# w_up: the tile endings cut into six one-engine steps, spread half a tile apart

## The chip, the core and the metric

The kernel runs on one core of one Trainium2 chip. Its time is device microseconds (us) from start to end of one execution. Before the change it is 2656.06 us, the median of three runs (2653.28, 2656.06 and 2662.95).

## What is computed

Two transformer-like blocks on x of 256 tokens by 2048 features, in fp32. Only one part of the first block matters here, the convolutional feed-forward layer:

```python
def _conv_ffn(h, w_up, conv_w, conv_b, w_down):
    u = h @ w_up                                # 256 x 2048 @ 2048 x 11264
    up = jnp.pad(u, ((0, 0), (CONV_WIDTH - 1, 0), (0, 0)))
    y = conv_b
    for j in range(CONV_WIDTH):                 # 3 taps along the tokens
        y = y + conv_w[j] * up[:, j:j + T]
    val, gate = jnp.split(y, 2, axis=-1)
    return (jax.nn.silu(gate) * val) @ w_down   # 256 x 5632 @ 5632 x 2048
```

## The kernel before, in words

**Weights.** Every large product streams its weights in pieces of 128 x 1024 fp32 values (512 KB). For each piece SyncE's queue (SP) issues a DMA into a raw buffer (L568). Then ACT writes the high half of the piece, rounded to fp32r (L587, through the helper `act`, L423), and DVE writes the low half, the piece less its high half (L588, through `tt`, L426). TensorE multiplies both. A program written by hand sets the order: `next` (L617) hands out a prepared piece and, before that, prepares pieces until four are ready, so that the piece prepared at one call is multiplied three calls later. A buffer ring of 13 slots (5 raw, 4 high, 4 low) serves the stream, so a new high half takes the slot of a piece that TensorE has just left.

Between the weight pieces of w_up and w_down the plan (`mix`, L533) lays 96 pieces of the modulation weights `w_ada`, two for every five. DVE alone works on those: one scalar_tensor_tensor (STT) of 128x1024 each (`_ada`, L628, through `stt`, L433). After each sixteen of them come a few small matmuls with the constant `con` (L763 to L778).

**w_up.** `block_ffn` (L1782) makes 88 tiles of 128 features by 256 tokens: 44 values j of the loop, each with i = 0 (the value) and i = 1 (the gate). `form_b` (L781) makes one tile from two pieces. A piece is 8 pairs of matmuls: the high weights on 512 columns (high and low input side by side) and the low weights on 256 columns. The 32 matmuls of a tile go into one PSUM bank, of which `pm` (L413) rotates three. The first two tiles come from `form_b2` (L798), which prepares the input at the same time.

**The ending of a tile** stands right behind its matmuls in the program, L1803 to L1814. It goes back and forth between two engines: ACT copies the upper 256 columns of the bank into `u`, DVE adds the lower 256 (`join`, L451); ACT makes `z`, the last tap with its bias (Identity, the only ACT operation of shape `s<-s,vec`); DVE adds the other two taps (STTs of 255 and 254 columns). For i = 1, ACT then takes the Silu and DVE multiplies into `act`. Each of the two engines carries out its instructions in the order of the program. So the high half that `next` makes for the following tile stands on ACT behind this ending, and the low half stands on DVE behind it. The working slot `y` is taken at each j and given back at the end of i = 1.

Around that, `bg` (L457) runs background generators (the rope tables early in w_up) and the late ends of `_ada`. After w_up comes w_down in the same function (L1823 on), in pieces of 24 matmuls of 512 columns, and later the second block, whose `win2` tiles use `form_b` too, with lighter endings.

Of the kernel before, what the change touches and what calls it, by code (L numbers as in the profile page):

```python
# [13 lines left out]
AF = mybir.ActivationFunctionType  # L14
ALU = mybir.AluOpType
# [4 lines left out]
T = 256  # L20
# [3 lines left out]
NFF = DFF // P  # L24
# [203 lines left out]
class Clock:  # L228
# [7 lines left out]
    def __init__(self):  # L236
        self.at = dict.fromkeys(("PE", "DVE", "ACT", "POOL", "SP"), 0.0)
        self.done, self.read = {}, {}
        self.columns = {}
        self.on = True  # L240
# [100 lines left out]
class Kern:  # L341
# [5 lines left out]
    def __init__(self, ctx, tc, a, out):  # L347
        self.clock = Clock()
        self.nc, self.a, self.out = Engines(self.clock, tc.nc), a, out
        self.timed = []  # L350
        p = self.const = ctx.enter_context(tc.tile_pool(name="const", bufs=1))
        self.vec = p.tile([P, NV], F32, name="vec")
        self.con = p.tile([P, NC_], F32, name="con")
        self.cs = p.tile([P, 32], F32, name="cs")
        self.mcol = p.tile([P, 6, 16], F32, name="mcol")
        self.scb = p.tile([P, 2, 16], F32, name="scb")
        self.mu1 = p.tile([P, 27], F32, name="mu1")
        self.ka1 = p.tile([P, 8], F32, name="ka1")
        self.st = p.tile([P, 16], F32, name="st")
        self.ssq = p.tile([P, 2, 2, 4], F32, name="ssq")  # L360
        self.epsr = p.tile([P, 2], F32, name="epsr")
        self.slots = ctx.enter_context(tc.tile_pool(name="slots", bufs=1))
        self.free_list = list(range(self.NSLOT))

        self.stream = list(range(self.NSLOT, self.NSLOT + self.RAW + self.HI + self.LO))
        self.used = []
        self.held = {}
        self.who, self.own, self.mixers = None, {}, []
        self.ps = ctx.enter_context(tc.tile_pool(name="ps", bufs=1, space=PSUM))
        self.ring_m, self.ring_g = [0, 1, 2], [3, 4, 5, 6]  # L370
        self.dram = ctx.enter_context(tc.tile_pool(name="dram", bufs=1, space=bass.MemoryType.DRAM))
        self.gens = []
        self.late = []
        self.flags = set()
# [242 lines left out]
    def next(self, name, lead=None, keep=False):  # L617
        if not keep:
            self.give(*self.used)
            self.used = []  # L620
        self.prefetch((self.lead if lead is None else lead) + 1)
        key, h, l = self.ready.pop(0)
        assert key == name, (key, name)
        self.used += [h, l]
        return h, l
# [155 lines left out]
    def form_b(self, name, nk, x):  # L781


        o = self.pm()
        for q in range(nk // 8):
            wh, wl = self.next(name)
            for kk in range(8):
                self.prod_b(o, wh, wl, x, kk, 8 * q + kk, nk)
            if q < nk // 8 - 1:
                self.bg()  # L790
        return o
# [429 lines left out]
    def step(self, g):  # L1221

        c = self.clock
        self.who = g[2]
        c.last = 0.0
        r = next(g[1], "end")
        self.who = None
        if r == "end":
            self.gens.remove(g)
            self.mixers.remove(g[2])  # L1230
        elif r == "wait":
            return False
        elif r != "go":
            g[0] = r or c.last
        return True
# [546 lines left out]
    def block_ffn(self):  # L1782
        nc = self.nc
        rs = self.st[:, 8:10]
        first, xs = self.form_b2("wup")
        x = self.by2(xs)
        act = [self.take() for _ in range(11)]
        av = self.at4(act)
        parts = {}

        def split(i):
            if i < 44:
                parts[i] = self.take(F32R), self.take(F32R)
                self.hl(*parts[i], act[i % 11])
                if i >= 33:
                    self.give(act[i % 11])

        for j in range(NFF):
            if j >= NFF - 2:
                split(j - NFF + 2)  # L1800
            y = self.take()
            for i in range(2):
                o = self.form_b("wup", 16, x) if j else first[i]  # L1803
                n = j + NFF * i
                z = y[:, i * T:(i + 1) * T]
                u = y[:, 512 + i * T:512 + (i + 1) * T]
                self.bg()
                self.join(u, o)
                self.act(z, u, AF.Identity, scale=self.v("cw2", n), bias=self.v("cb", n))
                self.stt(z[:, 1:], u[:, :T - 1], self.v("cw1", n), z[:, 1:], ALU.mult, ALU.add)  # L1810
                self.stt(z[:, 2:], u[:, :T - 2], self.v("cw0", n), z[:, 2:], ALU.mult, ALU.add)
            self.act(y[:, 512:768], y[:, T:512], AF.Silu)
            self.tt(av(j), y[:, 0:T], y[:, 512:768])
            self.give(y)  # L1814
            if j == 1:
                self.gens.append(self.rope_tables())
        self.give(*xs)
        gf = [self.take() for _ in range(2)]
        for h in range(2):
            nc.scalar.dma_start(out=gf[h], in_=self.a["nfg"][:, h * 1024:(h + 1) * 1024].to_broadcast([P, 1024]))  # L1820
        y = [self.take() for _ in range(4)]
        self.f = []
        for n in range(4):  # L1823
            o = [self.pm(), self.pm()]
            if n == 1:
                self.scale, self.shift = self.mod_affine("gpre", 5, 4)
            xh = lambda k: parts[11 * n + k // 4][0][:, (k % 4) * T:(k % 4 + 1) * T]
            xl = lambda k: parts[11 * n + k // 4][1][:, (k % 4) * T:(k % 4 + 1) * T]
            for q in range(22 if n < 3 else 18):
                i = 11 * n + q // 2  # L1830
                if (n, q) == (3, 14):
                    self.lend(-8)
                    self.lead = self.AHEAD
                if q % 2 == 0:
                    split(i + 2)
                wh, wl = self.next("wdn")
                self.piece_a(o, wh, wl, xh, xl, 2 * q, NFF)
                if q % 2:
                    self.give(*parts.pop(i))
                self.bg()  # L1840
            gate = lambda tt: self.add_gated(o, n, 5, tt, y, gf)
            if n == 2:
                self.warm(AF.Sqrt)
            if n < 3:
                gate(0)
                gate(1)
                self.turn_soon(y, n)

        self.y, self.rf = y, self.st[:, 4:6]

        def stats(tt):
            sl = slice(tt, tt + 1)
            vw = self.st[:, 0:2]
            nc.vector.tensor_reduce(out=vw, in_=self.ssq[:, :, tt], axis=AX.X, op=ALU.add)  # L1854
            v, w, e = vw[:, 0:1], vw[:, 1:2], self.st[:, 2:3]

            self.ts(e, v, EPS / D, EPS * EPS, ALU.mult, ALU.add)
            self.stt(w, w, 1.0 / D, e, ALU.mult, ALU.add)
            nc.vector.reciprocal(w, w)  # L1859
            self.act(rs[:, sl], w, AF.Sqrt)  # L1860
            self.diag(rs, tt)
            self.rstd(self.rf[:, sl], v, D)

        self.finish_a("wdn", o, xh, xl, NFF, gate, stats, lambda tt: self.turn(y[3], 3, self.scale, tt))
        for i in (42, 43):
            self.give(*parts.pop(i))
        self.give(self.row.pop((5, 0)), self.row.pop((5, 1)), *gf)
# [337 lines left out]
```

## Time and profile before

| | |
|---|---|
| median of 3 runs | 2656.06 us |
| the profiled execution's own time | 2659.07 us |
| its span in the profile | 2657.3 us |
| TensorE (PE) busy | 2552.5 us, 96% of the span |
| DVE busy | 1853.7 us, 70% |
| ACT busy | 1258.4 us, 47% |
| mean granted TensorE clock | 0.985 of full speed |

PE is the matmul side of TensorE and PEld its weight loads, which overlap the matmuls. The ends of matmuls in the profile are modelled and overlap one another; a high busy share of PE therefore does not say that it runs at its own pace. In a group of instructions the last part reads: busy us, mean ns of one, then the engine's idle time just before them and what ended most of it.

### The profile page before, as it was taken

How to read it: one execution, taken by the hardware profiler on the slowest of the kernel's cores; microseconds unless marked ns; L12 is line 12 of the kernel's file. 1: busy time of each engine (PE TensorE's matmuls, PEld its weight loads, DVE VectorE, ACT ScalarE, POOL GpSimd, SP SyncE). 2: the span in 40 equal slices, each digit the busy share in tenths (PEclk: the TensorE clock that was granted, in tenths of full speed). 3: DMA queues.
4: the chain of work that ended last, by engine and by line, in shares of the span. 5: the costliest groups of instructions: out<-in, count | busy, mean ns of one | idle time of the engine just before them, and what ended most of it. 6: DMA issues, size and time to landing. Idle time of an engine off the chain costs nothing.

```text
span 2657.3 us, 40136 instructions
## 1 busy us (share of the span) xinstructions
PE 2552.5 (96%) x15788; PEld 2119.8 (80%) x15788; DVE 1853.7 (70%) x2598; ACT 1258.4 (47%) x1923; POOL 89.1 (3%) x120
## 2 busy tenths in 40 slices
PE   6999999988999999999998999999999999999998
PEld 3777777667788888878887888888888888888887
DVE  3548955678788887888876556666787688566664
ACT  3363322345444444455665554444444444554443
POOL 0001032001000000000001000000000000000000
PEclk8999999998999999999998999999999999999999
DMA  9956764865677777777764654445666666555574
GB/s 372 388 171 208 265 210 160 280 201 174 236 239 255 240 249 236 247 270 269 267 217 146 200 193 156 143 151 198 216 202 215 222 200 199 181 187 189 190 242 143
DMA packets 168633, 579.65 MB, mean 218 GB/s; under 512 B 17914, under 2 KB 18298, under 8 KB 168444
## 3 DMA queue, kind: packets, MB, share of 16 engines
q1 hardware_dynamic: 163424, 561.88, 62.6%
q10 hardware_dynamic: 3916, 11.54, 1.3%
q0 software_dynamic: 1104, 3.67, 0.4%
q8 instruction: 123, 2.02, 0.3%
q14 instruction: 66, 0.54, 0.1%
HBM read 572.82 MB, written 4.19 MB: 217 GB/s over the span
## 4 chain that ended last, share of the span: by engine, by line
PE 55%; DVE 1%; ACT 0%; issue 0%; DVEq 0%; ACTq 0%
PE b L436 55%; PE b L439 1%; DVE s L426 0%; DVE s L433 0%; ACT s L423 0%; DVEq L2185 0%; ACT st L423 0%; DVE s L1875 0%; DVE st L430 0%; DVE s L430 0%; DVE st L916 0%; DVE st L1859 0%; DVE st L1854 0%; DVE st L433 0%; DVE st L1320 0%
## 5 line engine op out<-in xcount | busy, mean ns | idle before, releaser
L436 PE MATMUL b<-s,s 128*128 128x512 f32 (+1 forms) x10496 | 2010.1, 352 | 37.1 <-DVE s L426 23.2
L436 PEld LDWEIGHTS b<-s,s 128*128 128x128 f32 x10496 | 1688.1, 189 | 335.0 <-DVE s L426 38.2
L426 DVE TENSOR_TENSOR s<-s,s 128x1024 fp32r<-128x1024 f32 (+4 forms) x906 | 983.9, 1107 | 316.5 <-ACT s L423 299.8
L423 ACT ACTIVATE s<-s 128x1024 fp32r<-128x1024 f32 (+3 forms) x954 | 839.3, 913 | 481.2 <-PE b L436 170.4
L327 PE MATMUL b<-s,s 128*128 128x256 f32 (+6 forms) x4480 | 457.0, 306 | 48.4 <-DMA s<-in_w_ada 23.0
L327 PEld LDWEIGHTS b<-s,s 128*128 128x128 f32 (+3 forms) x4480 | 346.9, 159 | 154.0 <-issue 66.0
L423 ACT ACTIVATE s<-b 128x256 f32<-128x256 f32 (+2 forms) x338 | 134.3, 407 | 320.9 <-PE b L436 264.3
L426 DVE TENSOR_TENSOR s<-b,s 128x256 f32<-128x256 f32 (+1 forms) x324 | 143.7, 447 | 122.4 <-ACT s L423 100.0
L327 DVE TENSOR_TENSOR s<-s,s 128x1024 fp32r<-128x1024 f32 (+5 forms) x119 | 129.8, 1105 | 80.2 <-ACT s L327 76.6
L423 ACT ACTIVATE s<-s,vec 128x256 f32<-128x256 f32 x88 | 53.0, 602 | 224.8 <-DVE s L426 224.8
L327 ACT ACTIVATE s<-s 128x1024 fp32r<-128x1024 f32 (+6 forms) x112 | 108.1, 981 | 99.2 <-DVE s L327 37.0
L433 DVE SCALAR_TENSOR_TENSOR s<-s,cs,s 128x1024 f32<-128x1024 f32 x120 | 153.3, 1277 | 0.0
L327 ACT ACTIVATE s<-b 128x512 f32<-128x512 f32 (+1 forms) x105 | 52.5, 539 | 186.8 <-PE b L327 177.2
L433 DVE SCALAR_TENSOR_TENSOR s<-s,vec 128x255 f32<-128x255 f32 (+1 forms) x176 | 85.1, 484 | 62.1 <-ACT s L423 59.0
L327 DVE SCALAR_TENSOR_TENSOR s<-s,cs,s 128x1024 f32<-128x1024 f32 x51 | 65.7, 1288 | 14.1 <-DMA s<-in_w_ada 13.4
L426 DVE TENSOR_TENSOR s<-s 128x256 f32<-128x256 f32 x94 | 39.9, 425 | 26.9 <-ACT s L423 25.3
L426 POOL TENSOR_TENSOR s<-s,s 128x512 f32<-128x512 f32 x14 | 19.8, 1443 | 1014.3 <-ACT s L423 903.1
L433 DVE SCALAR_TENSOR_TENSOR s<-b,s 128x384 f32<-128x384 f32 x40 | 22.1, 553 | 36.6 <-PE b L436 36.6
L327 DVE TENSOR_TENSOR s<-b,s 128x256 f32<-128x256 f32 (+2 forms) x68 | 28.3, 465 | 24.8 <-PE b L327 20.9
L327 DVE TENSOR_TENSOR s<-s,b 128x512 f32<-128x512 f32 (+1 forms) x47 | 25.3, 559 | 20.0 <-PE b L327 19.7
L2039 POOL DMA_DIRECT2D s<-in_gpost x2 | 1.1, 533 | 1119.5 <-PE b L436 1119.5
L327 PEld LDWEIGHTS b<-con,s 128*128 128x128 f32 (+1 forms) x288 | 24.6, 158 | 9.8 <-ACT s L327 7.2
(115 smaller groups left out, 626.1 us busy)
## 6 DMA issues: line engine op xcount, KB each, us to landing
s<-in_win SPq DMA_DIRECT2D x302, 512.0 KB, 3.6
s<-in_w_ada SPq DMA_DIRECT2D x288, 512.0 KB, 5.0
s<-in_wup SPq DMA_DIRECT2D x176, 512.0 KB, 4.8
s<-in_wdn SPq DMA_DIRECT2D x88, 512.0 KB, 4.8
s<-in_win2v SPq DMA_DIRECT2D x48, 512.0 KB, 3.5
s<-in_wina SPq DMA_DIRECT2D x32, 512.0 KB, 10.6
s<-in_wout SPq DMA_DIRECT2D x32, 512.0 KB, 4.6
s<-in_wmp SPq DMA_DIRECT2D x32, 512.0 KB, 3.8
```

Of the source, the lines that this page charges most:

```text
L327: r = f(*a, **k)
L423: return self.nc.scalar.activation(out=out, in_=in_, func=func, **k)
L426: return (eng or self.nc.vector).tensor_tensor(out=out, in0=a, in1=b, op=op)
L433: return self.nc.vector.scalar_tensor_tensor(out=out, in0=a, scalar=s, in1=b, op0=op0, op1=op1)
L436: return self.nc.tensor.matmul(out, lhsT, rhs, start=start, stop=stop, skip_group_check=True)
L439: return self.nc.tensor.transpose(out, in_, self.c("ident"))
L2039: nc.gpsimd.dma_start(out=gg[h], in_=a["gpost"][:, h * 1024:(h + 1) * 1024].to_broadcast([P, 1024]))
```

## The change

The ending becomes a generator of six steps, each on one engine: 0 copy (ACT), 1 join's addition (DVE), 2 Identity (ACT), 3 the two STTs (DVE), and for i = 1 also 4 Silu (ACT) and 5 the multiplication (DVE). The tile loop only puts the generator on a list. `form_b` calls `step(True)` ahead of `next` and `step(False)` behind it, in each of its two pieces. `step(True)` moves every ending that is due a DVE step on by one, `step(False)` those that are due an ACT step; the older tile goes first, and no ending moves twice within one piece. As it works out, the ACT steps stand behind the high half of a tile's first piece, and the DVE steps ahead of the low half of its second piece. What is left of the endings after the last tile is put out in one go. The instructions themselves are the same, in number and shape.

```diff
         o = self.pm()
         for q in range(nk // 8):
+            if self.steps:
+                self.steps(True)
             wh, wl = self.next(name)
+            if self.steps:
+                self.steps(False)
             for kk in range(8):
                 self.prod_b(o, wh, wl, x, kk, 8 * q + kk, nk)
...
+        def ending(o, y, j, i):
+            n = j + NFF * i
+            z = y[:, i * T:(i + 1) * T]
+            u = y[:, 512 + i * T:512 + (i + 1) * T]
+            self.act(u, o[:, T:])
+            yield
+            self.tt(u, o[:, :T], u, ALU.add)
+            yield
+            self.act(z, u, AF.Identity, scale=self.v("cw2", n), bias=self.v("cb", n))
+            yield
+            self.stt(z[:, 1:], u[:, :T - 1], self.v("cw1", n), z[:, 1:], ALU.mult, ALU.add)
+            self.stt(z[:, 2:], u[:, :T - 2], self.v("cw0", n), z[:, 2:], ALU.mult, ALU.add)
+            yield
+            if i:
+                self.act(y[:, 512:768], z, AF.Silu)
+                yield
+                self.tt(av(j), y[:, 0:T], y[:, 512:768])
+                self.give(y)
+
+        def step(odd):
+
+            if odd:
+                now[0] += 1
+            for t in list(tails):
+                if t[0] % 2 == odd and t[1] < now[0]:
+                    t[0] += 1
+                    t[1] = now[0]
+                    if next(t[2], "end") == "end":
+                        tails.remove(t)
+
+        tails, now = [], [0]
+        self.steps = step
         for j in range(NFF):
...
             for i in range(2):
                 o = self.form_b("wup", 16, x) if j else first[i]
...
                 self.bg()
-                self.join(u, o)
...
-            self.act(y[:, 512:768], y[:, T:512], AF.Silu)
-            self.tt(av(j), y[:, 0:T], y[:, 512:768])
-            self.give(y)
+                tails.append([0, -1, ending(o, y, j, i)])
             if j == 1:
                 self.gens.append(self.rope_tables())
+        self.steps = None
+        while tails:
+            step(True)
+            step(False)
```

## Rows read from the trace of the kernel before

**Rows 1.** The page: busy shares of the engines, and PE in 40 slices

```profile
PE 2552.5 (96%) x15788; PEld 2119.8 (80%) x15788; DVE 1853.7 (70%) x2598; ACT 1258.4 (47%) x1923; POOL 89.1 (3%) x120
PE   6999999988999999999998999999999999999998
```

**Rows 2.** The DMA issues of w_up: durations, first and last start

```profile
L568 SPq DMA_DIRECT2D s<-in_wup x176: 327/328/1312, 578.6 to 1135.8; - x176
```

**Rows 3.** Busy us by stretch; three of w_up, one of win2 in block two

```profile
core 0: us, PE busy (x) PEld busy (x) DVE busy (x) ACT busy (x) POOL busy (x), PEclk, DMA share, GB/s
627.00:697.00 70.00, 63.43 (x342) 53.62 (x343) 57.56 (x87) 32.66 (x52) 0.00 (x0) 0.98 0.64 211
697.00:1127.00 430.00, 414.58 (x2306) 351.14 (x2305) 344.60 (x454) 211.31 (x319) 0.00 (x0) 1.00 0.73 246
1127.00:1165.00 38.00, 32.64 (x164) 26.31 (x164) 29.96 (x38) 21.02 (x29) 0.00 (x0) 1.00 0.68 229
1480.00:1580.00 100.00, 100.00 (x579) 87.49 (x578) 51.90 (x55) 51.08 (x75) 0.00 (x0) 1.00 0.60 190
```

**Rows 4.** Groups by form, 697 to 1127 us, DVE and ACT

```profile
L426 DVE TENSOR_TENSOR s<-s,s 128x1024 fp32r<-128x1024 f32 x142 | 170.2, 1224 | 16.2 <-ACT s L423 10.5 <-PE b L436 0.5
L423 ACT ACTIVATE s<-s 128x1024 fp32r<-128x1024 f32 x142 | 141.6, 1045 | 0.0
L433 DVE SCALAR_TENSOR_TENSOR s<-s,cs,s 128x1024 f32<-128x1024 f32 x54 | 69.0, 1279 | 0.0
L423 ACT ACTIVATE s<-s,vec 128x256 f32<-128x256 f32 x71 | 42.7, 602 | 179.3 <-DVE s L426 179.3
L433 DVE SCALAR_TENSOR_TENSOR s<-s,vec 128x255 f32<-128x255 f32 x71 | 34.4, 484 | 47.6 <-ACT s L423 47.6
...
L426 DVE TENSOR_TENSOR s<-b,s 128x256 f32<-128x256 f32 x71 | 29.7, 418 | 0.0
L423 ACT ACTIVATE s<-b 128x256 f32<-128x256 f32 x71 | 25.7, 361 | 0.1
L426 DVE TENSOR_TENSOR s<-s 128x256 f32<-128x256 f32 x35 | 14.9, 425 | 19.1 <-ACT s L423 19.1
L423 ACT ACTIVATE s<-s 128x256 f32<-128x256 f32 x35 | 14.6, 418 | 39.6 <-DVE s L433 39.6
```

**Rows 5.** The timeline of one ending (i = 1): start, us, engine, operation

```profile
812.99 0.42 DVE L426 TENSOR_TENSOR s<-b,s 128x256 f32<-128x256 f32 x1
...
813.44 0.60 ACT L423 ACTIVATE s<-s,vec 128x256 f32<-128x256 f32 x1 [2.85 <-DVE s L426]
814.07 1.00 DVE L433 SCALAR_TENSOR_TENSOR s<-s,vec 128x255 f32<-128x255 f32 x2 [0.67 <-ACT s L423]
815.17 2.32 ACT L423 ACTIVATE s<-s 128x256 f32<-128x256 f32 x3 [1.13 <-DVE s L433]
815.62 0.43 DVE L426 TENSOR_TENSOR s<-s 128x256 f32<-128x256 f32 x1 [0.54 <-ACT s L423]
816.57 1.23 DVE L426 TENSOR_TENSOR s<-s,s 128x1024 fp32r<-128x1024 f32 x1 [0.53 <-ACT s L423]
```

**Rows 6.** Groups by form, 697 to 1127 us, PE

```profile
L436 PE MATMUL b<-s,s 128*128 128x512 f32 x1133 | 401.2, 397 | 2.2 <-ACT s L423 2.2
L436 PEld LDWEIGHTS b<-s,s 128*128 128x128 f32 x2265 | 346.3, 188 | 77.7 <-DVE s L426 23.8 <-ACT s L423 4.4 <-issue 1.0
L436 PE MATMUL b<-s,s 128*128 128x256 f32 x1133 | 322.4, 285 | 13.2 <-DVE s L426 13.1
...
L436 PE MATMUL b<-s,con 128*128 128x512 f32 x8 | 3.8, 592 | 0.0
L436 PE MATMUL b<-con,s 128*128 128x1 f32 x32 | 3.7, 245 | 0.0
```

**Rows 7.** The timeline: PE's waits at the start of w_up and entering w_down

```profile
626.24 0.51 PE L436 MATMUL b<-s,s 128*128 128x512 f32 x1 [1.26 <-ACT s L423]
...
627.50 4.74 PE L436 MATMUL b<-s,s 128*128 128x256 f32 x17 [0.76 <-DVE s L426]
...
1148.76 11.02 PE L436 MATMUL b<-s,s 128*128 128x256 f32 x51 [2.33 <-DVE s L426]
...
1160.85 0.73 PE L436 MATMUL b<-s,s 128*128 128x512 f32 x2 [1.06 <-ACT s L423]
...
1162.30 8.01 PE L436 MATMUL b<-s,s 128*128 128x512 f32 x34 [0.72 <-DVE s L426]
```

More of the change, by code (lines that the diff above doesn't have):

```diff
@@ L1803, in block_ffn @@
                 o = self.form_b("wup", 16, x) if j else first[i]
-                n = j + NFF * i
-                z = y[:, i * T:(i + 1) * T]
-                u = y[:, 512 + i * T:512 + (i + 1) * T]
                 self.bg()
-                self.join(u, o)
-                self.act(z, u, AF.Identity, scale=self.v("cw2", n), bias=self.v("cb", n))
-                self.stt(z[:, 1:], u[:, :T - 1], self.v("cw1", n), z[:, 1:], ALU.mult, ALU.add)
-                self.stt(z[:, 2:], u[:, :T - 2], self.v("cw0", n), z[:, 2:], ALU.mult, ALU.add)
-            self.act(y[:, 512:768], y[:, T:512], AF.Silu)
-            self.tt(av(j), y[:, 0:T], y[:, 512:768])
-            self.give(y)
+                tails.append([0, -1, ending(o, y, j, i)])
             if j == 1:
                 self.gens.append(self.rope_tables())
+        self.steps = None
+        while tails:
+            step(True)
+            step(False)
         self.give(*xs)
```

## The prediction, made before the changed kernel ran

> **What bounds the kernel now.** I read the page first: PE is busy in 96% of the span, DVE in 70% [rows 1]. That would leave a change on DVE and ACT nothing to win, but PE's busy time is modelled, so the question is whether PE runs at its own pace inside w_up. The stage lasts about 557 us by its DMA issues [rows 2], a fifth of the span.
>
> PE's own pace shows where the same tiles run with nothing to wait for: in win2, 1480 to 1580 us, PE is busy for all of the 100 us, DVE for 52, and 579 matmuls start [rows 3]. A tile is 32 matmuls, so its price is 32 x 100 / 579 = 5.53 us. In w_up from 697 to 1127 us there are 71 Identity operations, one to a tile [rows 4], hence 430 / 71 = 6.06 us a tile, at the same granted clock of 1.00 [rows 3]. So 0.53 us a tile is lost although PE's row says 96% busy.
>
> DVE says where it goes. It works 344.6 us there, 4.85 a tile [rows 3]. It waits for ACT three times: 47.6 us for the Identity, 19.1 for the Silu, 10.5 for the high half [rows 4], together 77.2 us or 1.09 a tile. The rest, 8.2 us, is 0.11 a tile. 4.85 + 1.09 + 0.11 = 6.05: **DVE's work and its waits fill the tile**, and PE waits for DVE's low halves. One ending shows the pattern [rows 5]: join, 0.67 us idle until the Identity is there, two STTs, 0.54 idle until the Silu is there, then 0.53 until the high half, which stood on ACT behind that Silu. ACT in turn waits 179.3 us for the joins, 2.5 a tile [rows 4]. The two engines play one ball at a time, though neither is full.
>
> **The change, part by part.** Nothing is added or removed: per tile one copy, join, Identity and two STTs, per two tiles one Silu and one multiplication, with the durations of [rows 4]. The steps hold no DMA and pass none; SP's issues go on following the low halves that free a raw slot. POOL has no part in it.
>
> *DVE's waits.* Each DVE step now stands one piece, some 2.8 us at PE's pace, behind the ACT step that feeds it, and that gap holds a low half. Behind the end of a tile's matmuls ACT runs the high half, Silu, Identity and copy, 1045 + 418 + 602 + 361 ns = 2.43 us [rows 4], all put out before DVE's batch. DVE meanwhile does the low half of the first piece (1.22, from 1.05 on), then multiplication (0.43) and STTs (0.97) of older tiles, and comes to the join at about 3.7 us or later, when the copy is 1.3 us old. So I cost the three waits at nothing. That cover is gone only if DVE has nothing left to do, and then its idling costs nothing either. What is late next is PE itself: DVE needs 4.85 + 0.11 = 4.96 us, PE 5.53. This reserve of 0.57 us makes the result robust: over half of the waits could stay and PE would still set the time. A modulation piece in a heavy tile makes DVE's sum 2 x 1.224 + 0.418 + 0.967 + 0.425 + 1.279 = 5.54 us, still about PE's 5.53.
>
> *The added lateness.* A bank is free after the join, which moves half a tile back. Three banks rotate, so it is wanted two tiles after the next one begins, and the join stands on DVE ahead of the low half that the matmuls into that bank need anyway: no new wait. The low half behind DVE's batch is wanted four pieces, 11.1 us, after the tile's end; it is done about 2.43 + 0.42 + 1.28 + 1.22 = 5.4 us after it, at most 6.8 with the STTs and multiplication last. At least 4.3 us are spare. The slot `y` is held over three values of j in place of one; I cost it at nothing, as 37 slots are shared out at build time and a slot reused that late is long read.
>
> *The sum*, in three stretches, against the profiled execution.
> Middle, 697 to 1127 us: 430 - 71 x 5.53 (392.4) - 7.5 of matmuls with `con` [rows 6] = 30.1 us. The ends: 15.4 us, the idle time that PE's rows admit (2.2 + 13.2) [rows 6], and 37.6, if the 7.5 were hidden. PEld's idle is nearer to the middle: 77.7 us [rows 6], while at PE's own pace 578 loads leave 12.5 of 100 us idle [rows 3], which is 49 for 2265, so 28.7 are excess. I take 30.1.
> Start, 627 to 697: 343 loads are 10.7 tiles, 59.2 us at PE's pace. DVE has more to do there (57.6 us busy in 70 [rows 3], the rope tables among it) plus 1.2 of small gaps, and the endings of the first two tiles, 2 x 0.42 + 4 x 0.48 + 0.43 = 3.2 us, move in. DVE sets 62.0 us: gain 8.0, and some 1.5 of the waits of 1.26 and 0.76 just before [rows 7]. I take 9.5, between 6.6 (PE not busy) and 12.3 (PE's pace and the waits).
> Entry to w_down, 1127 to 1165: waits of 2.33, 1.06 and 0.72 = 4.1 us [rows 7] are DVE's arrears and go. The last endings still come in one chain of the length of today's; an older Silu and Identity, 1.0 us, may stand ahead of the last copy. I take 3.1, between 0 and 5.4 (38 less 32.6 busy [rows 3]).
> Together **42.7 us**, between 22 and 55. The profiled execution took 2659.07 us, 1.8 over its span and 3.0 over the median. 2659.1 - 42.7 = 2616.4; on the median's footing **2613 us**.
>
> **A rule weighed.** In [rows 4] ACT waits 2.5 us a tile at the Identity and does nothing else: the high half behind it is not drawn ahead. [...]
>
> **The rivals.**
> *Half the waits stay.* ACT's Silu, Identity and copy stand behind a high half that waits for a slot PE must leave; if DVE then still waits 0.85 us a tile, the tile is 5.81, the gain 0.24 x 82 tiles and a little at both ends, some 23 us: 2633. For it: the chain of 2.43 us starts only at PE's end. Against: the spare 1.3 us worked out above. Chance 0.10.
> *The wait only changes its place.* DVE waits its 1.09 us in one piece at the join, and the change does not do what it says: 2656. Chance 0.04.
> *Slower.* In the second piece DVE's join stands ahead of the low half, and DVE waits there for ACT's whole 2.43 us in place of 1.09: 1.34 x 82 = 110 us more, 2766. It decides once DVE waits there for more than 1.09 us a tile, and PE feels it only if fewer than about one and a half prepared pieces lie ahead (4.3 us spare of 11.1). At w_up's beginning there is no such lead, but there PE waits, so its tile has long ended when the join comes up. Chance 0.03.
> *PE has more in it.* [...] Chance 0.02. [...]
>
> **How the numbers follow.** The forecast has the chance that is left, 0.81. Its bounds reach from 2601 to 2634; the range 2602 to 2632 leaves out the two upper rivals, the lowest one and most of the half gain. About 0.5%, 13 us, is what a measurement of this kernel can tell from no change. Faster by more: forecast, half gain and quick PE, 0.93; within: 0.04; slower: 0.03.
>
> **What would show it.** In w_up PE near 100% busy and 5.5 to 5.7 us between Identities; ACT's 179 us of waits for joins gone; DVE's waits in front of high halves, not Identity or Silu, without PE waiting; the last w_up DMA issued near 1096 in place of 1136 us; w_down and block two as long as now. Waits of PE for DVE's low halves of over 10 us in the middle of w_up, or DVE waiting for copies ahead of joins, would make the prediction wrong.

## The result, and the profile after

The changed kernel takes 2611.98 us (median of 4 runs, 2607.56 to 2614.72) against 2655.18 us before, measured with it: a ratio of 0.983, 95% interval 0.9806 to 0.9855. It is faster by 43.2 us. The profiled execution has a span of 2612.9 us, 44.4 less than that of before.

First three stretches that answer to [rows 3], from the view of busy time by stretch (columns as there), the kernel after:

```profile
627.00:697.00 70.00, 70.00 (x398) 60.67 (x397) 66.00 (x100) 39.25 (x60) 0.00 (x0) 1.00 0.79 262
697.00:1086.00 389.00, 389.00 (x2206) 336.65 (x2206) 323.02 (x433) 206.40 (x307) 0.00 (x0) 1.00 0.78 259
1440.00:1540.00 100.00, 100.00 (x576) 87.31 (x575) 53.53 (x58) 51.42 (x75) 0.00 (x0) 1.00 0.61 190
```

In w_up PE is now busy for all of the 70 and the 389 us, as it is in win2, and the traffic from 697 us on is 259 GB/s in place of 246. The groups by form of the same stretch answer to [rows 4] and [rows 6]; the line numbers have moved by one:

```profile
L437 PEld LDWEIGHTS b<-s,s 128*128 128x128 f32 x2166 | 332.0, 188 | 51.2 <-ACT s L424 0.5 <-issue 0.5
L437 PE MATMUL b<-s,s 128*128 128x256 f32 x1083 | 304.1, 281 | 0.0
L427 DVE TENSOR_TENSOR s<-s,s 128x1024 fp32r<-128x1024 f32 x135 | 165.3, 1224 | 55.9 <-ACT s L424 53.0
L424 ACT ACTIVATE s<-s 128x1024 fp32r<-128x1024 f32 x137 | 145.3, 1061 | 184.8 <-PE b L437 163.1 <-ACT s L424 12.1 <-issue 7.4
...
L424 ACT ACTIVATE s<-s,vec 128x256 f32<-128x256 f32 x68 | 39.9, 586 | 0.0
...
L434 DVE SCALAR_TENSOR_TENSOR s<-s,vec 128x255 f32<-128x255 f32 x68 | 32.5, 478 | 0.0
L427 DVE TENSOR_TENSOR s<-b,s 128x256 f32<-128x256 f32 x68 | 28.4, 418 | 0.0
...
L427 DVE TENSOR_TENSOR s<-s 128x256 f32<-128x256 f32 x34 | 14.2, 419 | 0.0
```

DVE's wait for the Identity (47.6 us before) and for the Silu (19.1) are gone, and so are ACT's 179.3 us of waits for joins. The joins (`s<-b,s`) do not wait either. What is left of DVE's idle time stands almost wholly in front of low halves, 53.0 us, for the high half from ACT, and ACT in turn waits 163.1 us for PE to leave a slot: both engines now wait for PE. PE hardly waits for them (in front of weight loads 0.5 us for ACT; 23.8 for DVE and 4.4 for ACT before).

One tile's share of the timeline shows how (start, us, engine, operation; [rows 5] is its counterpart):

```profile
800.81 1.23 DVE L427 TENSOR_TENSOR s<-s,s 128x1024 fp32r<-128x1024 f32 x1 [0.73 <-ACT s L424]
800.99 0.59 ACT L424 ACTIVATE s<-s,vec 128x256 f32<-128x256 f32 x1
801.48 0.36 ACT L424 ACTIVATE s<-b 128x256 f32<-128x256 f32 x1
801.95 0.42 DVE L427 TENSOR_TENSOR s<-s 128x256 f32<-128x256 f32 x1
...
802.29 0.99 DVE L434 SCALAR_TENSOR_TENSOR s<-s,vec 128x255 f32<-128x255 f32 x2
...
803.20 0.42 DVE L427 TENSOR_TENSOR s<-b,s 128x256 f32<-128x256 f32 x1
803.58 1.23 DVE L427 TENSOR_TENSOR s<-s,s 128x1024 fp32r<-128x1024 f32 x1
804.73 1.28 DVE L434 SCALAR_TENSOR_TENSOR s<-s,cs,s 128x1024 f32<-128x1024 f32 x1
```

While DVE makes a low half, ACT makes an Identity and a copy beside it. DVE then runs a multiplication, two STTs and a join of three different tiles without a gap; the copy had ended at 801.84, 1.36 us before the join began.

**Where the time went.** The small matmuls with `con` that follow every sixteen modulation pieces are fixed points of the program, 20 tiles apart. Their starts in the two traces, with the first matmul of w_up and the first of w_down, give this table (us):

| from, to | before | after | saved |
|---|---|---|---|
| start of the execution, first w_up matmul | 602.6 | 600.1 | 2.5 |
| first w_up matmul, first con group | 132.8 | 118.6 | 14.2 |
| 20 tiles | 121.9 | 114.8 | 7.1 |
| 20 tiles | 121.9 | 114.8 | 7.1 |
| 20 tiles | 120.7 | 114.8 | 5.9 |
| fourth con group, first w_down matmul | 51.5 | 46.2 | 5.3 |
| first w_down matmul, fifth con group | 67.7 | 65.3 | 2.4 |
| fifth con group, near the end of w_down | 180.4 | 180.4 | 0.0 |

So 42.0 us come from w_up and the entry to w_down, nothing from the rest of w_down. The 2.5 us ahead of w_up are in code that the change leaves alone. w_up's own DMA issues, to be set beside [rows 2], take 516.6 us in place of 557.2:

```profile
L569 SPq DMA_DIRECT2D s<-in_wup x176: 327/328/1157, 576.1 to 1092.7; - x176
```

### The profile page after: what moved, and what is told of

Read it like the earlier page. It is cut to its first block, busy times and chain, and to the rows that moved or that the text cites. A ratio compares the mean times of both kernels' runs of the same rounds, so it can differ in the third digit from the quotient of the medians.

```text
span 2612.9 us, 40253 instructions
## 1 busy us (share of the span) xinstructions
PE 2535.5 (97%) x15788; PEld 2117.4 (81%) x15788; DVE 1845.6 (71%) x2598; ACT 1262.2 (48%) x1923; POOL 89.4 (3%) x120
## 4 chain that ended last, share of the span: by engine, by line
PE 77%; DVE 1%; ACT 0%; issue 0%; DVEq 0%; ACTq 0%
PE b L437 76%; PE b L440 1%; DVE s L427 0%; DVE s L434 0%; ACT s L424 0%; ACT st L424 0%; DVEq L2218 0%; DVE s L431 0%; DVE st L431 0%; DVE s L1908 0%; DVE st L921 0%; DVE st L1892 0%; DVE st L434 0%; DVE st L1887 0%; DVE st L1325 0%
## 5 line engine op out<-in xcount | busy, mean ns | idle before, releaser
L424 ACT ACTIVATE s<-s 128x1024 fp32r<-128x1024 f32 (+3 forms) x954 | 849.5, 915 | 659.6 <-PE b L437 363.6
L424 ACT ACTIVATE s<-s,vec 128x256 f32<-128x256 f32 x88 | 51.5, 587 | 1.6 <-DVE s L427 1.6
L327 DVE TENSOR_TENSOR s<-b,s 128x256 f32<-128x256 f32 (+2 forms) x68 | 28.3, 464 | 25.4 <-PE b L327 21.0
L327 PEld LDWEIGHTS b<-con,s 128*128 128x128 f32 (+1 forms) x288 | 23.8, 156 | 9.9 <-ACT s L327 7.2
```

The source lines that it names most:

```text
L327: r = f(*a, **k)
L424: return self.nc.scalar.activation(out=out, in_=in_, func=func, **k)
```

## The experiments

The theory: DVE's waits for ACT inside an ending, 1.09 us a tile on top of 4.96 us of work and gaps, made the tile's 6.06 us; cutting the ending apart removes them, and PE sets the tile after that. The rivals: it is the later place of the ending and not its cutting; each microsecond of DVE's waits or work counts in full; the places beside the halves matter; the lead of prepared pieces carries nothing.

### The ending as late, but whole

```diff
-            for t in list(tails):
-                if t[0] % 2 == odd and t[1] < now[0]:
...
+            for t in [] if odd else list(tails):
+                for _ in t[2]:
+                    pass
+                tails.remove(t)
```

> The changed kernel, but each ending is put out whole and unsplit, copy to multiplication in one go, behind the halves of the following tile's first piece. Theory (the gain is DVE's waits for ACT inside an ending, 1.09 us a tile, which only the splitting takes away; TensorE at 5.53 us a tile is the new bound): the three waits are back, 47.6 us for the Identity and 19.1 for the Silu per 71 tiles as before, and the time is that of before, 2645 to 2660. Rival (the gain is the later place, because the next halves are prepared ahead of the ending): 2608 to 2617.

Measured: 2655.79 us, ratio to before 1.000 (0.9988 to 1.0013). The groups by form of this run, 697 to 1086 us:

```profile
L437 PE MATMUL b<-s,s 128*128 128x256 f32 x1023 | 291.7, 285 | 13.0 <-DVE s L427 12.8
L427 DVE TENSOR_TENSOR s<-s,s 128x1024 fp32r<-128x1024 f32 x128 | 153.5, 1224 | 15.5 <-ACT s L424 10.9
...
L434 DVE SCALAR_TENSOR_TENSOR s<-s,vec 128x255 f32<-128x255 f32 x64 | 31.0, 484 | 42.9 <-ACT s L424 42.9
...
L427 DVE TENSOR_TENSOR s<-s 128x256 f32<-128x256 f32 x32 | 13.6, 426 | 17.7 <-ACT s L424 17.7
```

The three waits are back with the sizes of before, (42.9 + 17.7 + 10.9) / 64 = 1.12 us a tile, and with them the whole time. The later place alone gains nothing.

### One of the three waits put back

```diff
             self.tt(u, o[:, :T], u, ALU.add)
-            yield
             self.act(z, u, AF.Identity, scale=self.v("cw2", n), bias=self.v("cb", n))
-            yield
             self.stt(z[:, 1:], u[:, :T - 1], self.v("cw1", n), z[:, 1:], ALU.mult, ALU.add)
```

> The changed kernel, but join, Identity and STTs stand together in the DVE step ahead of the second piece's low half, so DVE waits about 0.67 us a tile for the Identity again and perhaps 0.1 more for the high half; the Silu and the multiplication stay apart. Theory (DVE has a reserve of 0.57 us a tile under TensorE): DVE 4.96 + 0.67 to 0.77 = 5.63 to 5.73 us against 5.53 and the con matmuls, so little of the gain goes: 2612 to 2626. Rival (every microsecond of DVE's wait counts in full, the gain is in proportion to the wait removed): 0.42 of 1.09 us removed, 2655 - 0.39 x 43 = 2638, 2633 to 2645.

Measured: 2616.08 us, ratio 0.9853 (0.9839 to 0.9868). From the groups by form, 697 to 1086 us:

```profile
L437 PE MATMUL b<-s,s 128*128 128x256 f32 x1089 | 305.5, 281 | 0.0
...
L424 ACT ACTIVATE s<-s,vec 128x256 f32<-128x256 f32 x69 | 41.5, 602 | 146.9 <-DVE s L427 146.9
L434 DVE SCALAR_TENSOR_TENSOR s<-s,vec 128x255 f32<-128x255 f32 x69 | 33.4, 484 | 46.3 <-ACT s L424 46.3
```

DVE again waits 0.67 us a tile for the Identity, and in this stretch PE does not notice. ACT waits for the joins again too, 146.9 us, so its waits cost nothing by themselves. What such a wait of DVE cost here was not its length, 46.3 us in this stretch, but what of it passed DVE's reserve under PE. The 4 us to the changed kernel lie at the two ends. From the first w_up matmul to the first con group it takes 122.6 us in place of 118.6, and PE waits there for low halves, 3.2 us in five waits, of which this is the longest:

```profile
656.81 5.91 PE L437 MATMUL b<-s,s 128*128 128x256 f32 x32 [1.33 <-DVE s L427]
```

From the fourth to the fifth con group it takes 113.9 us in place of 111.5. In the third 20 tiles 2.1 us come back (112.7 in place of 114.8), by a change of PE's pace that the last section describes.

### The old place, the Identity's work given to DVE

```diff
-                self.act(z, u, AF.Identity, scale=self.v("cw2", n), bias=self.v("cb", n))
+                self.ts(z, u, self.v("cw2", n), self.v("cb", n), ALU.mult, ALU.add)
```

> The kernel before, endings in their old place, with the last tap and bias as one TENSOR_SCALAR on DVE in place of the Identity on ACT: DVE works some 0.35 to 0.45 us a tile more and waits 0.67 less. Theory (DVE's work and waits add up to the tile): tile 4.96 + 0.40 + 0.42 = 5.78 us, 0.28 x 82 = 23 us off 2655: 2622 to 2642. Rival (the share of work on DVE counts, the waits run beside something else): slower by 0.4 x 88, about 2690.

Measured: 2635.62 us, ratio 0.9928 (0.9913 to 0.9943). The stretch 697 to 1086 us, and in it the first of the two STTs, which stood behind the Identity, and DVE's new operation:

```profile
697.00:1086.00 389.00, 383.08 (x2157) 328.89 (x2156) 349.73 (x493) 165.57 (x235) 0.00 (x0) 1.00 0.76 255
```

```profile
L433 DVE SCALAR_TENSOR_TENSOR s<-s,vec 128x255 f32<-128x255 f32 x67 | 32.5, 484 | 2.4
L430 DVE TENSOR_SCALAR s<-s,vec 128x256 f32<-128x256 f32 x67 | 27.7, 413 | 2.4
```

DVE works 0.41 us a tile more, its share rises from 80% to 90% (349.73 / 389), and the kernel is 20 us faster, because the 0.67 us of waiting in front of the STTs is gone. DVE's work and waits add up, as the theory has it: 20 tiles take 117.4 us, 5.87 a tile, where it forecast 5.78.

### ACT's steps on the other side of the high half

```diff
             if self.steps:
                 self.steps(True)
+            if self.steps:
+                self.steps(False)
             wh, wl = self.next(name)
-            if self.steps:
-                self.steps(False)
```

> The changed kernel with ACT's steps ahead of the first piece's high half in place of behind it, all else equal. Theory (a distance of one piece covers the hand-off, whichever side of the half the steps stand on): 2608 to 2617, TensorE without waits in the middle of w_up. Rival (the places beside the halves are what does it): the high half comes 1.4 us later each tile, DVE waits for it, and half the gain or more goes, 2630 to 2655.

Measured: 2611.71 us, ratio 0.9826 (0.9808 to 0.9845). The stretch 697 to 1086 us:

```profile
697.00:1086.00 389.00, 389.00 (x2219) 338.24 (x2218) 325.42 (x436) 211.77 (x307) 0.00 (x0) 1.00 0.79 261
```

PE is busy for all of it. Of the two places that the change chose, ACT's behind the high half is not needed. The place of DVE's steps ahead of the low half was not varied, and neither was the distance of one piece, but the first two runs, which took the distance out in whole or in part, say what it is worth.

### More and less work on DVE in the changed kernel

Once or twice more, with a scalar that holds zero:

```diff
             self.stt(z[:, 2:], u[:, :T - 2], self.v("cw0", n), z[:, 2:], ALU.mult, ALU.add)
+            self.stt(z[:, 1:], u[:, :T - 1], self.epsr[:, 1:2], z[:, 1:], ALU.mult, ALU.add)
```

> The changed kernel with one more STT of 128x255 on DVE per tile, behind the two taps, that adds zero times u: 0.48 us a tile. Theory (TensorE sets the tile at 5.53 us and DVE has 0.57 us of reserve): DVE 4.96 + 0.48 = 5.44, still under TensorE: 2608 to 2619. Rival (DVE sets w_up in the changed kernel too, only with fewer waits): 0.48 x 88 = 42 us more, 2645 to 2660.

> The same with two such STTs, 0.97 us a tile. Theory: DVE 4.96 + 0.97 = 5.93 us passes TensorE's 5.53 and its 0.1 of con matmuls, 0.30 to 0.40 us a tile over 84 tiles, 25 to 34 us more: 2632 to 2648, with TensorE waiting for low halves again and DVE hardly idle. Rival (DVE sets it anyway): 85 us more, 2690 to 2700. Third (neither; another resource hides it): 2608 to 2619.

And with one tap left out:

```diff
-            self.stt(z[:, 1:], u[:, :T - 1], self.v("cw1", n), z[:, 1:], ALU.mult, ALU.add)
```

> The changed kernel without the STT of the middle tap (128x255), which leaves out one of the three taps of the convolution and frees 0.48 us of DVE a tile. Theory (TensorE is the bound): no gain, 2605 to 2616. Rival (DVE still sets w_up): 0.48 x 88 = 42 us less, 2565 to 2580.

Measured: one more 2614.44 us (0.9847, 0.9827 to 0.9868), two more 2638.57 (0.9935, 0.9918 to 0.9951), one less 2614.74 (0.9844, 0.9828 to 0.986). The stretch 697 to 1086 us of each, one more first:

```profile
697.00:1086.00 389.00, 389.00 (x2218) 338.14 (x2218) 357.40 (x509) 207.32 (x309) 0.00 (x0) 1.00 0.78 264
```

```profile
697.00:1086.00 389.00, 384.78 (x2165) 329.71 (x2164) 376.32 (x561) 202.98 (x300) 0.00 (x0) 1.00 0.75 256
```

```profile
697.00:1086.00 389.00, 389.00 (x2206) 336.61 (x2205) 291.88 (x366) 206.03 (x306) 0.00 (x0) 1.00 0.77 259
```

DVE's busy share goes from 75% (291.88 / 389) over 83% in the changed kernel and 92% to 97% (376.32), and the time stays level until the last. With two more DVE has almost no idle time, PE waits for low halves again, and 20 tiles take 117.1 and 117.6 us in the first two of those cycles, 5.87 a tile. Of PE's low-half matmuls in that run:

```profile
L437 PE MATMUL b<-s,s 128*128 128x256 f32 x1062 | 300.6, 283 | 4.2 <-DVE s L427 3.4
```

The bend lies between 0.48 and 0.97 us of added work. The wait of 0.67 us put back, which cost the same 20 tiles nothing, puts it above 0.67, a little past the prediction's reserve of 0.57 us. That settles which engine bounds w_up after the change: PE.

### A shorter lead

```diff
         self.steps = step
+        self.lead = 0
         for j in range(NFF):
...
         self.steps = None
+        self.lead = self.LEAD
```

> The changed kernel with pieces prepared at the call that hands them out in w_up's loop (lead 0 in place of 3), so that the low half behind the join is wanted one piece, 2.8 us, after the tile's end and not four, 11.1. Theory (the lead of three pieces is what covers DVE's wait at the join, and it decides once the lead is under one and a half pieces): copy 0.36, join 0.42, high half and low half make the low half ready about 2.7 us after the tile's end, 3.3 with a modulation piece between, so TensorE waits 0 to 0.6 us in many tiles: 5 to 40 us more, 2617 to 2652, with waits of TensorE for the low halves. Rival (the lead carries nothing): 2605 to 2616. The slower rival of the prediction, in full: 2700 or more.

> The changed kernel with lead 1 in w_up's loop: the low half behind the join is wanted two pieces, 5.5 us, after the tile's end. With lead 0 the time was 2654 with TensorE waiting for low halves. Theory (the lead decides only where what is wanted of DVE after the tile's end, some 3.3 us with a modulation piece, does not fit into it; under one and a half pieces by the prediction): 5.5 us is enough in the middle of w_up, TensorE waits hardly there; something may be lost behind the con matmuls and at the entry to w_down, where less is ready: 2606 to 2628. Rival (each piece of lead is worth the same): between 2612 and 2654 by two thirds, 2640 or more.

Measured: lead 0 2654.17 us (0.9991, 0.9981 to 1.0), just over the range that I gave the theory; lead 1 2619.66 us (0.9854, 0.9837 to 0.987), inside. The timeline of lead 0 behind a con group:

```profile
726.66 0.69 DVE L427 TENSOR_TENSOR s<-b,s 128x512 f32<-128x512 f32 x1 [5.46 <-PE b L437]
...
731.30 3.09 PE L437 MATMUL b<-s,s 128*128 128x256 f32 x16 [3.59 <-DVE s L427]
```

the stretch behind the same wait at the next con group (the last three figures are PE's granted clock, DMA share and GB/s):

```profile
852.60:855.80 3.20, 3.20 (x12) 2.72 (x12) 1.67 (x4) 0.00 (x0) 0.00 (x0) 0.50 0.00 0
```

and lead 1 at the entry to w_down:

```profile
1113.36 0.42 DVE L427 TENSOR_TENSOR s<-b,s 128x256 f32<-128x256 f32 x1 [2.12 <-ACT s L424]
...
1118.50 1.22 PE L437 MATMUL b<-s,s 128*128 128x512 f32 x2 [2.84 <-ACT s L424]
```

```profile
1113.00:1125.00 12.00, 8.94 (x26) 6.34 (x25) 9.10 (x11) 8.02 (x10) 0.00 (x0) 0.72 0.57 185
```

With lead 0 PE waits 0.20 to 0.26 us in front of low halves, as expected, but only seven times in 20 tiles, 1.7 us together. What I had left out are the modulation pieces' late ends: DVE's addition behind a con group waits 5.46 us for PE, the low half stands behind it, and PE then waits 3.59 us. At such waits behind the second, third and fourth con group PE's granted clock was 0.50 (from 852.5 to 855.9, 972.0 to 978.8 and 1094.9 to 1101.7 us); behind the first it stayed at 1.00. So most of the 7.4 us that 20 tiles lose (122.2 in place of 114.8) lies behind the con groups. At the entry to w_down PE waits 5.59 us.

With lead 1 no wait of PE is left inside w_up: from its first matmul to w_down's it takes 509.4 us, with lead 3 509.2, with lead 0 546.5. It loses its time at the entry to w_down, 71.7 us in place of 65.3 from there to the fifth con group. 2.84 of it is the wait shown, and PE's granted clock is 0.72 from 1113 to 1125 us, where it is 1.00 from 1110 to 1122 in the changed kernel.

So inside w_up a low half wanted two pieces after the tile's end is early enough, and one piece after it is not. The steps' lateness does use up the lead, for with lead 0 the 64 joins from 697 to 1086 us waited 44.0 us for their copies, 0.69 a tile. How much of the 42 us it cost is not shown: the kernel before was not run with a shorter lead, and the late ends behind con groups are in it as well.

## Why the prediction was right

**The bound.** The tile of before was read as DVE's work plus its waits, 4.85 + 1.09 + 0.11 us, with PE at 5.53 underneath. The whole late ending (waits back, time back) and the tap on DVE (more work, less waiting, 20 us gained) show that reading; one STT less, one more and two more show that PE bounds it afterwards.

**The waits at nothing.** The cover was named as the low half, the STTs and the multiplication of older tiles, the join coming 1.3 us after the copy; the timeline has 1.36. The DVE waits that are left, 53.0 us, stand in front of low halves and cost nothing, as was said.

**The reserve of 0.57 us.** It was smaller than what the runs showed, so the argument stood on the safe side. A wait of 0.67 us put back left 20 tiles at 114.8 us, 0.48 us of added work did too, and 0.97 us did not (117.1 and 117.6). With PE's measured 5.74 us a tile in place of 5.53 the reserve is 5.74 - 4.96 = 0.78 us, which lies between them. It does not cover the two ends of w_up, where the 0.67 us cost their 4 us.

**The sum.** 42.7 us were forecast, 42.0 are found between the same points. Its three terms were less exact than their sum, which came out so close because their errors cancel; that part is luck. Brought to the table's stretches by 30.1 / 71 = 0.42 us a tile, they were 9.5 + 2.7 = 12.2 for the start (measured 14.2), 60 x 0.42 = 25.4 for the three times 20 tiles (20.1), and 3.1 + 1.9 = 5.0 for the end (7.7). The **middle** was mis-sized: its term took PE's price from win2, 5.53 us and 0.11 of con matmuls, 5.64 us together. Measured are 114.8 / 20 = 5.74, just above the 5.5 to 5.7 us that were named as the sign. PE's pace itself made the difference (last section); in the three runs in which it changed, the third 20 tiles took 112.7 us, which is 5.64 a tile. Against that stands the **end**: the charge of 1.0 us for an older Silu and Identity ahead of the last copy did not fall due. In the timeline the Identity ahead of it starts at 1108.01 us and the last copy at 1109.51, when PE is done; the chain of copy, join, Identity, STTs, Silu and multiplication then runs to 1114.15, and PE works through w_down's prepared pieces all the while. Another 1.3 us is what PE stood idle there beyond the three waits that I had counted, 38 - 32.6 - 4.1 ([rows 3] and [rows 7]); after the change PE is busy for all of 1086 to 1120 us. At the **start** I had let DVE set the time, 62.0 us against 59.2 at PE's pace. But from 627 to 697 us PE is busy throughout, starts 398 matmuls in place of 342, and DVE is busy for 66.0 us of the 70. The granted clock there is 1.00 in place of 0.98. So the term's upper end, PE's pace and the waits, 12.3 + 2.7 = 15.0, was nearer to the 14.2.

**The rivals.** Half the waits staying: in length they nearly did. DVE still waits 53.0 us for high halves, 0.78 a tile, against the rival's 0.85. But these high halves wait for PE, so DVE spends there what it has to spare. With a wait inside the ending put back the time was 2616, not 2633, since its 0.67 us lie within the reserve of the middle. The wait in a new place: no, the joins stand without idle time in front of them. Slower: what it says of the lead is borne out, as it decides between one and two pieces and w_up has four between a tile's end and the low half behind its join. Its price is not: with lead 0 the joins waited 0.69 us a tile, and the time was 2654, not 2766. PE with more in it: no, after the change w_up's tile took 5.74 us, slower than win2's 5.53 and 0.11 of con matmuls, 5.64 together; where PE kept to the quicker of its two paces (last section), the tile took just those 5.64.

**The weighed rule.** On both engines a half stayed behind an instruction that waited. Before the change ACT's 179.3 us of idle time for joins stood in front of Identities, and 0.0 us in front of the high halves behind them ([rows 4]); in the lead-0 run the low half, started at 730.02 us, stood on DVE behind an addition that waited 5.46 us for PE and started at 726.66.

## What to carry to other kernels

Where two engines hand a tile back and forth, each in the order of its program, as ACT and DVE did here, add each engine's busy time and its waits for the other, per tile; if that sum is the tile's time (for DVE before the change 4.85 + 1.09 + 0.11 of 6.06 us), the hand-offs bound the stage although both engines look part idle (DVE was busy for 80% of it and ACT for 49%). Put each hand-off a piece apart, so that other tiles' work lies between, and pay for the added lateness out of the buffers and prepared pieces that are there already. Work out the next bound first: it caps the gain, and it tells how much of the waits may stay (here 0.67 of the 1.09 us a tile, at no cost in the middle of w_up).

## What the runs showed that was not expected

At a granted clock of 1.00 PE's pace was not one number. From the starts of neighbouring matmul records, the step from a 512-column matmul to the next one is 230 to 233 ns in win2 of both kernels (1480 to 1580 us before, 1440 to 1540 after). In w_up after the change it is 232 to 241 ns, 236 on the mean, up to the fourth con group at 1063 us, and 230 on the mean behind it, with no wait in the records. It did not hang on whether ACT or DVE was busy at the time: 236 ns on the mean with both busy, 237 with neither.

From the first con group on, in the runs in which PE did not wait, the pace kept to one of the two values from one con group to the next. With ACT's steps ahead it was 230 ns from 625 us to the first group, 236 to the third, 230 to the fourth and 236 behind it. The runs with the wait put back and with one more STT had 230 ns between the third and the fourth group as well, and in all three the third 20 tiles took 112.7 us after 114.8 twice. So 2 us between two of these runs may be PE's pace and not the edit. The cause stays open.
